# A decoder block on one core: attention scores over all 128 rows, another order within the attention step, query halves, and other buffers for some weights

## The chip, the core and the metric

The kernel runs on one core of a Trainium2 chip. A core has a matrix engine (TensorE, in the profile PE, its weight loads PEld), a vector engine (VectorE, DVE), a scalar engine (ScalarE, ACT), GpSimd (POOL) and a queue that issues transfers (SyncE, SP). The metric is the device time of one execution in microseconds. The kernel before takes 1441.95 us, the median of three runs (1440.77 to 1442.16).

## What is computed

One decoder layer on 1024 tokens of width 1024, in float32:

```python
u = rmsnorm(x, norm_mix_w)
proj = u @ w_in + b_in
cb, cc, cx, q, k, v, g_conv, g_attn = split(proj)
y_conv = (cb * causal_dwconv(cc * cx, conv_mix_w)) @ w_conv_out
q, k = apply_rope(q, cos, sin), apply_rope(k, cos, sin)
y_attn = sliding_window_attention(q, k, v, sinks) @ w_attn_out + b_attn_out
x = x + (sigmoid(g_conv) * y_conv + sigmoid(g_attn) * y_attn) @ w_mix_out
u = rmsnorm(x, norm_ffn_w)
up, gate = split(u @ w_ffn_up)
x = x + (silu(causal_dwconv(up, ffn_conv_w, ffn_conv_b)) * gate) @ w_ffn_down
return rmsnorm(x, norm_final_w)
```

The attention has 8 query heads of 64 channels and 2 key heads, blocks of 128 queries that see their own and the previous block of keys, a mask inside these 256 keys, and a learned sink per head in the denominator:

```python
scores = where(valid, q @ k.T * scale, -inf)
m = maximum(max(scores), sink)
p = exp(scores - m)
probs = p / (sum(p) + exp(sink - m))
```

## The kernel before, in words

Every float32 product is made from two parts of each operand: the first is the value rounded to the matrix engine's format (ScalarE copies it), the second the remainder (VectorE subtracts). `mm3` (L142) multiplies first by first, first by second and second by first, so a product of a 128 by 128 weight block with 512 tokens is three matmuls. The stages follow each other: an opening with norm, transposes of u and the first parts of the key and query projections; the rest of the projections for q, k and v; the attention; its output projection (`ya`); the other input projections, the convolution's and the gates' (`Pairs`, with sums of blocks so that seven products do the work of eight); the convolution's output (`yc`); the mixing product; and the feed-forward part.

In the opening the order of all engines is written out by hand. `load_x` asks for a block of 128 tokens, `rows_of` norms it, `cols_of` transposes it and splits it into u's parts, `part` multiplies a quarter of the tokens, `turn_on(n)` does the next n instructions of the tables for the rotary embedding on VectorE and GpSimd, `keep_warm` are matmuls of zeros.

Queries lie in two tiles `qs[0]` and `qs[1]`, one per key head g. A tile holds on the 64 rows of its own head the first parts and on the other 64 rows the second parts of the same queries, for four heads of the group (c). `ks[g]` holds the first parts of its keys twice, on both row halves. So one matmul over 128 rows gives first by first and second by first. The remaining term, first parts of the queries by second parts of the keys, is a matmul over the 64 own rows with `kl`, one tile whose two halves belong to the two key heads (L444 and L445).

The attention has 16 steps, one for each query block n and key head g (`Step`). What a step does is spread over three turns of the loop, and the order of TensorE, ScalarE and VectorE in it is again written by hand (`manual_schedule`). In turn i TensorE computes the scores of step i + 1, the transposes of the probabilities of step i, half of a filler (a product of the input projection that fills the time, 24 matmuls, L144 to L146) and the values of step i. VectorE takes the maxima of step i + 1 head by head (L451, with the reading of the accumulator), negates all four (L454), adds the sinks (L455), totals step i - 1 (L495), takes the second parts of the probabilities (L139 with `pl`), stores the second parts of the output (L139 with `qs`), and norms step i + 1 (L465 to L467); in every second turn it also takes the second parts of the next filler's weights. ScalarE computes the first parts (`ph`), the exponentials (L460, one per head, and L461 for the sink), the rest of the output (L491), its first parts, and in every second turn a filler's eviction (L430) and weights.

Tiles come from pools: `act` has 16 buffers of 4 KB per row, `tmp` 2, `rawp` 2 for weights as they land, `ps` 4 accumulators of two banks. An instruction that needs a buffer waits for the last reader of what was in it. SP issues its transfers in order, so one that waits for a buffer holds those behind it. Outside the hand-written stretches a scheduler sets the order; `issue_after` puts an instruction behind a given one. `tail_in` loads the convolution's output weights (`load_co`) and the z tiles (`load_z`) during the last products of the input projections.

## Time and profile before

| what | value |
|---|---|
| median of three runs | 1441.95 us |
| profiled execution, its own time | 1441.58 us |
| its span | 1439.8 us |
| TensorE busy | 1418.2 us (98%) |
| VectorE busy | 1003.6 us (70%) |
| ScalarE busy | 562.5 us (39%) |
| GpSimd busy | 85.7 us (6%) |
| mean granted clock of TensorE | 0.997 of full speed |

The span goes from the first to the last instruction, and the execution's own time includes what lies around it. Busy time is the time in which at least one instruction of the engine runs. [...] In a list of waits a row names who waited, for what, and how long in total.

### The profile page before, as it was taken

The numbers are of one execution on the slowest core, as the hardware profiler recorded it, in microseconds if no ns is written. First come the engines' busy times: TensorE is split into PE (matmuls) and PEld (weight loads), VectorE is DVE, ScalarE is ACT, GpSimd is POOL, SyncE is SP. The second block draws the span as 40 slices with busy tenths as digits, with TensorE's granted clock in tenths as the row PEclk, the third lists the DMA queues.
The fourth block names the chain that finished last, engine by engine and source line by source line (L and its number), as shares of the span: only waits on it lengthen the run. The fifth ranks groups of instructions, "written<-read, shape, count | busy, mean of one in ns | idle before, by whom it ended". The sixth has DMA issues, their size and how long they took to land.

```text
span 1439.8 us, 17099 instructions
## 1 busy us (share of the span) xinstructions
PE 1418.2 (98%) x6447; PEld 1164.9 (81%) x6447; DVE 1003.6 (70%) x1511; ACT 562.5 (39%) x897; POOL 85.7 (6%) x144
## 2 busy tenths in 40 slices
PE   8999999999999999999999999999999999999997
PEld 6987777788888888877888878888888888888886
DVE  7575676856788787545644697787777777655567
ACT  5545555623333333232323543333333334444343
POOL 5210000000000000000000000000000000000000
PEclk9999999999999999999999999999999999999999
DMA  5320000242455554255552222222232225797603
GB/s 217 89 59 30 30 16 30 88 161 74 161 205 205 191 185 178 76 177 196 184 174 103 74 98 107 101 105 95 88 110 93 99 94 197 275 377 256 195 31 146
DMA packets 68450, 193.18 MB, mean 134 GB/s; under 512 B 8144, under 2 KB 8400, under 8 KB 68368
## 3 DMA queue, kind: packets, MB, share of 16 engines
q1 hardware_dynamic: 53280, 139.64, 28.8%
q0 software_dynamic: 14368, 51.13, 9.2%
q10 hardware_dynamic: 720, 1.33, 0.3%
q8 instruction: 50, 0.82, 0.2%
q14 instruction: 32, 0.26, 0.1%
HBM read 136.75 MB, written 52.69 MB: 132 GB/s over the span
## 4 chain that ended last, share of the span: by engine, by line
PE 86%; DVE 6%; DMA 5%; ACT 2%; issue 1%; SPq 0%; DVEq 0%; ACTq 0%
PE xup L649 8%; PE zup L649 8%; PE yup L649 8%; PE dna L1151 8%; PE dnb L1151 6%; PE yin L649 5%; PE xin L649 5%; PE zin L649 5%; PE wup L649 4%; PE win L649 3%; PE ps_fill L144 3%; PE ps_fill L146 3%; PE ps_fill L145 3%; PE mx L145 2%; PE mx L146 2%; PE mx L144 2%
## 5 line engine op out<-in xcount | busy, mean ns | idle before, releaser
L1138 DVE TENSOR_TENSOR pd<-rd,pd 128x1024 fp32r<-128x1024 f32 x77 | 93.7, 1222 | 54.1 <-ACT pd L1141 50.3
L627 ACT CAST pup<-sup 128x512 fp32r<-128x512 f32 x80 | 47.8, 620 | 203.2 <-DVE sup L613 203.2
L1141 ACT CAST pd<-rd 128x1024 fp32r<-128x1024 f32 x77 | 80.6, 1053 | 104.1 <-PE dnb L1151 37.1
L1151 PE MATMUL dna<-pd 128*128 128x512 f32 x528 | 120.3, 389 | 0.0
L1151 PEld LDWEIGHTS dna<-pd 128*128 128x128 f32 x528 | 99.1, 188 | 20.5
L1151 PE MATMUL dnb<-pd 128*128 128x512 f32 x396 | 90.2, 389 | 0.0
L1151 PEld LDWEIGHTS dnb<-pd 128*128 128x128 f32 x396 | 74.3, 188 | 15.4
L649 PE MATMUL zin<-u,pin 128*128 128x512 f32 x360 | 86.1, 389 | 0.0
L627 ACT CAST pin<-sin 128x512 fp32r<-128x512 f32 x52 | 31.1, 620 | 135.3 <-DVE sin L613 126.4
L649 PEld LDWEIGHTS zin<-u,pin 128*128 128x128 f32 x360 | 67.6, 188 | 14.0
L630 DVE TENSOR_TENSOR pup<-sup,pup 128x512 fp32r<-128x512 f32 x80 | 53.6, 689 | 18.5 <-ACT pup L627 15.0
L144 PE MATMUL ps_fill<-u,w_fill 128*128 128x512 f32 x160 | 64.0, 400 | 0.0
L146 PE MATMUL ps_fill<-u,w_fill 128*128 128x512 f32 x160 | 62.5, 391 | 0.0
L145 PE MATMUL ps_fill<-u,w_fill 128*128 128x512 f32 x160 | 62.3, 389 | 0.0
L649 PE MATMUL yup<-b22h,pup 128*128 128x512 f32 x176 | 57.9, 390 | 0.9 <-DVE aup L665 0.9
L649 PE MATMUL zup<-b11h,pup 128*128 128x512 f32 x176 | 57.8, 390 | 0.0
L649 PE MATMUL zup<-b21h,pup 128*128 128x512 f32 x176 | 57.7, 389 | 0.0
L451 DVE CUSTOM_DVE_ANT_0 p<-s,cst_sb,pcol_sb 128x256 f32<-128x256 f32 x64 | 27.2, 480 | 37.2 <-PE s L445 34.6
L649 PE MATMUL yup<-bt1h,pup 128*128 128x512 f32 x160 | 52.5, 389 | 0.0
L649 PE MATMUL wup<-bt2h,pup 128*128 128x512 f32 x160 | 52.5, 389 | 0.0
L649 PE MATMUL xup<-bt3h,pup 128*128 128x512 f32 x160 | 52.5, 389 | 0.0
L649 PE MATMUL xup<-bt4h,pup 128*128 128x512 f32 x160 | 52.5, 389 | 0.0
(361 smaller groups left out, 3470.4 us busy)
## 6 DMA issues: line engine op xcount, KB each, us to landing
rup<-in_w_up SPq DMA_DIRECT2D x44, 512.0 KB, 3.5
rin<-in_w_in SPq DMA_DIRECT2D x30, 512.0 KB, 6.7
td<-in_w_down SPq DMA_DIRECT2D x22, 512.0 KB, 5.3
tsp<-td POOLq DMA_DIRECT2D x22, 512.0 KB, 3.7
rd<-tsp SPq DMA_DIRECT2D x44, 256.0 KB, 5.3
rd<-in_w_down SPq DMA_DIRECT2D x33, 256.0 KB, 5.3
rd<-hs SPq DMA_DIRECT2D x33, 256.0 KB, 3.7
x<-in_x SPq DMA_DIRECT2D x16, 512.0 KB, 3.7
```

The costliest lines, as they stand in the source:

```text
L144: nc.tensor.matmul(dst, ah, bh, start=first, stop=False)
L145: nc.tensor.matmul(dst, ah, bl, start=False, stop=False)
L146: nc.tensor.matmul(dst, al, bh, start=False, stop=last)
L451: nc.vector.tensor_tensor_reduce(out=self.p[:, c], in0=self.s[:, c], in1=masks[0 if self.n == 0 else 1], scale=SCALE, scalar=pc(COL_SINK + ...
L627: nc.scalar.copy(self.parts[p, q][:, 0], src())
L630: v.tensor_sub(t[:, 1], src(), t[:, 0].bitcast(F32))
L649: nc.tensor.matmul(dst, a, b[:, kc], start=first and i == 0, stop=last and i == 2, skip_group_check=p >= PLAIN and more)
L1138: v.tensor_sub(t[:, 2:], raws_d[n - 1], t[:, :2].bitcast(F32))
L1141: nc.scalar.copy(parts_d[n][:, :2], raws_d[n])
L1151: nc.tensor.matmul(sets[side, i], t[:, s, tok], t[:, b], start=g == 0 and k == 0 and not more, stop=g == NG - 1 and k == 2, skip_group_che ...
```

## The change

Scores: `kl` becomes two tiles, one per key head, whose other 64 rows GpSimd fills with zeros; the second score matmul runs over all 128 rows with the same stationary queries as the first. The first gate block is written to DRAM after its eviction and read again behind the attention. Query block 0 has no previous keys: its transposes, parts and values go over one block of keys in place of two. Queries lie in two halves of 512 tokens, and the first two blocks of the output projection are multiplied half by half. In the step, each head's maximum is followed by its negation, the exponentials of the next step stand ahead of the first parts, and the norms ahead of the second parts. The last filler's product moves into the hand-written order, and sums that the scheduler had put ahead of the last total are issued behind the attention. The convolution's output weights 1 to 3 and the first z tiles land in `act` buffers, the weights asked for earlier. In the opening, loads, table work and parts change their places.

```diff
@@ opening (order written out by hand) @@
         load_x(0)
+        load_x(1)
...
-        load_x(1)
...
         raw_k = load_unit(w_in[U_K], "k")
+        raw_q0 = load_unit(w_in[U_Q], "q0")
...
-        turn_on(2)
         rows_of(0)
-        turn_on(1)
         rows_of(1)
+        turn_on(8)
         cols_of(0, False)
         keep_warm(N_WARM[1])
+        early["k"] = split_unit(raw_k, "k", eng=nc.gpsimd)
         cols_of(0, True)
-        early["k"] = split_unit(raw_k, "k", eng=nc.gpsimd)
-        turn_on(5)
         cols_of(1)
+        turn_on(20)
...
-    qs = [mid(f"qs{g}", F32R) for g in range(2)]
+    qs = [mid(f"qs{g}", F32R, (P, 2, 4, 512)) for g in range(2)]
     ks = [act(f"ks{g}", F32R) for g in range(2)]
-    kl = act("kl", F32R)
+    kl = [act(f"kl{g}", F32R) for g in range(2)]
+    for g in range(2):
+        nc.gpsimd.memset(kl[g][other[g]].bitcast(F32), 0.0)
...
-            split(k[own[g]], ks[g][own[g]], kl[own[g]])
+            split(k[own[g]], ks[g][own[g]], kl[g][own[g]])
...
+    gsp0 = dram.tile([P, T], F32, name="gsp0")
...
+        nc.scalar.activation(filled[f], ps_fill[f], AF.Identity, bias=pc(COL_BIN + col))
+        if f == 0:
+            nc.gpsimd.dma_start(gsp0, filled[f])
...
+            self.blocks = 2 if self.n else 1
...
             for c in range(4):
-                nc.tensor.matmul(self.s[:, c], qs[g][:, c, self.queries], ks[g][:, kc], start=True, stop=False)
-                nc.tensor.matmul(self.s[:, c], qs[g][rows, c, self.queries], kl[rows, kc], start=False, stop=True)
+                nc.tensor.matmul(self.s[:, c], qs[g][:, self.h, c, self.queries], ks[g][:, kc], start=True, stop=False)
+                nc.tensor.matmul(self.s[:, c], qs[g][:, self.h, c, self.queries], kl[g][:, kc], start=False, stop=True)
...
-            nc.vector.tensor_scalar_mul(st[:, 1], st[:, 0], -1.0)
+                nc.vector.tensor_scalar_mul(st[:, 1, c:c + 1], st[:, 0, c:c + 1], -1.0)
...
-            for k2 in range(2):
+            for k2 in range(self.blocks):
...
-        def split(self):
+        def first_parts(self):
             self.hl = [act(f"p{x}{self.name}", F32R, (P, 2, 4, P)) for x in "hl"]
-            split(self.pt, *self.hl)
+            nc.scalar.copy(self.hl[0][:, :self.blocks], self.pt[:, :self.blocks])
+        def second_parts(self):
+            hi, lo = [x[:, :self.blocks] for x in self.hl]
+            nc.vector.tensor_sub(lo, self.pt[:, :self.blocks], hi.bitcast(F32))
...
+            n = 2 * self.blocks
+            for i in range(n):
...
-            step.split()
             if nxt:
                 nxt.exps()
+            step.first_parts()
             fill_part(f, h, range(KC))
-            if nxt is st[-1]:
+            if nxt:
                 nxt.norms()
+            step.second_parts()
             if prev:
                 prev.store()
-            if nxt and nxt is not st[-1]:
-                nxt.norms()
...
+        nc.vector.scalar_tensor_tensor(filled[8], ps_fill[9], pc(COL_BIN + U_X), filled[8], op0=ALU.add, op1=ALU.mult)
         st[-1].rest()
...
+    gas[0] = act("ga0")
+    nc.sync.dma_start(gas[0], gsp0)
...
-            next(gen_in)
-            next(gen_in)
+            with tc.issue_after(after_attention):
+                next(gen_in)
+                next(gen_in)
...
+        yas = [ps(f"ya{2 * q + jj}") for jj in range(2)]
+        for jj, h in [(jj, h) for h in range(2) for jj in range(2)] if q == 0 else [(jj, h) for jj in range(2) for h in range(2)]:
+            for c in range(4):
+                f = slice((jj * 4 + c) * P, (jj * 4 + c + 1) * P)
+                mm3(yas[jj][:, halves[h]], wa[q][0][:, f], wa[q][1][:, f], qs[0][:, h, c], qs[1][:, h, c], c == 0, c == 3)
...
+    def fetch_co(n):
+        raws_co[n] = act(f"raw_co{n}")
+        nc.sync.dma_start(raws_co[n], w_co[n // 2, n % 2])
...
-        for f in {0: [lambda: load_co(0)], 1: [lambda: load_z(0, 0)], 2: [lambda: load_z(0, 1)], 3: [lambda: load_co(1)],
-                  5: [lambda: load_co(2)], 6: [lambda: load_z(0, 2), lambda: load_z(0, 3)], 7: [lambda: load_co(3)]}.get(m, ()):
+        for f in {0: [lambda: load_co(0)], 1: [lambda: load_z(0, 0), lambda: fetch_co(1)], 2: [lambda: load_z(0, 1), lambda: fetch_co(2)],
+                  3: [lambda: load_co(1)], 4: [lambda: fetch_co(3)],
+                  5: [lambda: load_co(2), lambda: load_z(0, 2)], 6: [lambda: load_z(0, 3)], 7: [lambda: load_co(3)]}.get(m, ()):
```

VectorE, from the last maximum of a turn to the store of the output, in the kernel before (p are the probabilities, sm the statistics of the step's four heads, pt the transposed probabilities, pl their second parts, os and o the output):

```order
L451 ISA p_1195,sm_1196<-s_1175,cst_sb,pcol_sb 128x256
L451 ISA sm_1196 128x1
L454 TENSOR_SCALAR sm_1196<-sm_1196 128x4
L455 TENSOR_TENSOR sm_1196<-sm_1196,pcol_sb 128x4
L495 TENSOR_TENSOR os_1184<-o_1170,os_1184 64x512
L139 TENSOR_TENSOR pl_1205<-pt_1186,ph_1204 128x1024
L139 TENSOR_TENSOR qs_705<-os_1184,qs_704 64x4x128
L465 TENSOR_TENSOR sm_1196<-sm_1196 128x4
L466 RECIPROCAL sm_1196<-sm_1196 128x4
L467 TENSOR_TENSOR p_1195<-p_1195,sm_1196 128x1024
```

The same stretch of VectorE in the changed kernel, from the third head on:

```order
L457 ISA p_1276,sm_1277<-s_1254,cst_sb,pcol_sb 128x256
L457 ISA sm_1277 128x1
L460 TENSOR_SCALAR sm_1277<-sm_1277 128x1
L457 ISA p_1276,sm_1277<-s_1254,cst_sb,pcol_sb 128x256
L457 ISA sm_1277 128x1
L460 TENSOR_SCALAR sm_1277<-sm_1277 128x1
L461 TENSOR_TENSOR sm_1277<-sm_1277,pcol_sb 128x4
L506 TENSOR_TENSOR os_1265<-o_1249,os_1265 64x512
L471 TENSOR_TENSOR sm_1277<-sm_1277 128x4
L472 RECIPROCAL sm_1277<-sm_1277 128x4
L473 TENSOR_TENSOR p_1276<-p_1276,sm_1277 128x1024
L487 TENSOR_TENSOR pl_1294<-pt_1267,ph_1293 128x1024
```

The three rows of the norms (L465 to L467 before, L471 to L473 now) moved from behind the store to ahead of the second parts, and a negation of one column stands behind every head.

ScalarE, from the rest of an output to the first parts of the stored one in the kernel before (ph are the first parts of the probabilities):

```order
L491 COPY os_1263<-o_1245 64x512
L138 CAST ph_1283<-pt_1265 128x1024
L460 ACTIVATE p_1274,sm_1275<-p_1274,sm_1275 128x256 x4
L461 ACTIVATE sm_1275<-sm_1275 128x4
L138 CAST qs_704<-os_1263 64x4x128
```

The same five rows of ScalarE's step in the changed kernel, with its line numbers:

```order
L502 COPY os_1265<-o_1249 64x512
L466 ACTIVATE p_1276,sm_1277<-p_1276,sm_1277 128x256 x4
L467 ACTIVATE sm_1277<-sm_1277 128x4
L483 CAST ph_1293<-pt_1267 128x1024
L138 CAST qs_704<-os_1265 64x4x128
```

The exponentials of the next step moved ahead of the first parts of this one.

## Rows read from the trace of the kernel before

**Rows 1.** The page: busy us, share of span, instructions; then the chain's shares.

```profile
PE 1418.2 (98%) x6447; PEld 1164.9 (81%) x6447; DVE 1003.6 (70%) x1511; ACT 562.5 (39%) x897; POOL 85.7 (6%) x144
...
PE 86%; DVE 6%; DMA 5%; ACT 2%; issue 1%; SPq 0%; DVEq 0%; ACTq 0%
```

**Rows 2.** Waits of TensorE: line, releaser, us in total, times, longest.

```profile
PE tp_a L182 <- DVE y_a L172: 3.6, 4, 1.6
PE yc L144 <- ACT co L138: 1.9, 1, 1.9
...
PE ya L144 <- ACT qs L138: 1.0, 1, 1.0
```

**Rows 3.** Stretches: us, busy by engine (instructions), granted clock, DMA share, GB/s.

```profile
0.00:20.00 20.00, 13.91 (x65) 7.76 (x66) 12.94 (x30) 10.97 (x18) 6.32 (x9) 1.00 0.78 286
...
160.00:180.00 20.00, 20.00 (x92) 15.45 (x91) 14.03 (x37) 11.12 (x27) 0.00 (x0) 1.00 0.11 34
```

**Rows 4.** Timeline of TensorE, one attention step: start, us, engine, line, operation.

```profile
146.74 0.28 PE L444 MATMUL s<-ks,qs 128*128 128x256 f32 x1
146.95 0.38 PE L445 MATMUL s<-kl,qs 64*128 64x256 f32 x1
147.26 0.38 PE L444 MATMUL s<-ks,qs 128*128 128x256 f32 x1
...
149.13 1.09 PE L473 MATMUL pt<-cst_sb,p 128*128 128x128 f32 x8
149.98 0.48 PE L144 MATMUL ps_fill<-u,w_fill 128*128 128x512 f32 x1
...
155.53 0.39 PE L483 MATMUL o<-ph,vs 128*128 128x512 f32 x1
```

**Rows 5.** Chain of waits, one query part in the opening: start, us, count.

```profile
36.30 2.87 PE ps_q L288 x24
```

**Rows 6.** Timeline of the weight loads in the same stretch.

```profile
36.03 2.94 PEld L288 LDWEIGHTS ps_q<-u,w_q 128*128 128x128 f32 x24
```

**Rows 7.** Timeline of VectorE in the step before that of rows 4.

```profile
140.74 0.48 DVE L451 CUSTOM_DVE_ANT_0 p<-s,cst_sb,pcol_sb 128x256 f32<-128x256 f32 x1
141.15 0.08 DVE L451 DVE_READ_ACCUMULATOR2_ANT sm<- 128x1 f32 x1
141.27 0.17 DVE L454 TENSOR_SCALAR sm<-sm 128x4 f32<-128x4 f32 x1
141.47 0.16 DVE L455 TENSOR_TENSOR sm<-sm,pcol_sb 128x4 f32<-128x4 f32 x1
141.66 0.69 DVE L495 TENSOR_TENSOR os<-o,os 64x512 f32<-64x512 f32 x1
142.39 1.23 DVE L139 TENSOR_TENSOR pl<-pt,ph 128x1024 fp32r<-128x1024 f32 x1
144.38 0.69 DVE L139 TENSOR_TENSOR qs<-os,qs 64x512 fp32r<-64x512 f32 x1 [0.77 <-ACT qs L138]
145.08 0.16 DVE L465 TENSOR_TENSOR sm<-sm 128x4 f32<-128x4 f32 x1
...
145.50 1.22 DVE L467 TENSOR_TENSOR p<-p,sm 128x1024 f32<-128x1024 f32 x1
```

**Rows 8.** Timeline of VectorE in the opening: two small instructions.

```profile
9.40 0.15 DVE L156 TENSOR_SCALAR st_a<-ss_a 128x1 f32<-128x1 f32 x1
9.47 0.16 DVE L157 RECIPROCAL st_a<-st_a 128x1 f32<-128x1 f32 x1
```

**Rows 9.** Groups of the attention stretch, by form: the exponentials; mean ns.

```profile
L460 ACT ACTIVATE p<-p,sm 128x256 f32<-128x256 f32 x64 | 31.8, 499 | 6.3 <-DVE sm L454 6.2
```

**Rows 10.** Timeline of VectorE behind the attention.

```profile
271.00 2.35 DVE L740 TENSOR_TENSOR ta<-u 128x1024 f32<-128x1024 f32 x2
...
275.65 0.69 DVE L495 TENSOR_TENSOR os<-o,os 64x512 f32<-64x512 f32 x1
```

**Rows 11.** DMA issues near the convolution's output weights: count, KB, us to landing.

```profile
raw_co<-in_w_co SPq DMA_DIRECT2D x7, 512.0 KB, 3.6
```

More of the change, by code (lines that the diff above doesn't have):

```diff
@@ L324, in hybrid_kernel @@
         nc.sync.dma_start(cst_sb[:, CST_MASK:], cst[:, CST_MASK:])
+        early["q0"] = split_unit(raw_q0, "q0")
         rows_of(2)
-        turn_on(20)
-        early["q0"] = split_unit(raw_q0, "q0")
+        part("k", 0)
         rows_of(3)
-        part("k", 0)
+        part("q0", 0)
         cols_of(2)
@@ L332, in hybrid_kernel @@
         rows_of(4)
-        part("q0", 0)
         cols_of(3)
+        part("q1", 0)
         rows_of(5)
-        part("q1", 0)
+        cols_of(4)
         part("k", 1)
-        cols_of(4)
         rows_of(6)
+        cols_of(5)
         part("q0", 1)
-        cols_of(5)
         rows_of(7)
-        turn_on(4)
+        cols_of(6)
         part("q1", 1)
-        part("k", 2)
-        cols_of(6)
-        turn_on(7)
-        part("q0", 2)
         cols_of(7)
         turn_on()
+        part("k", 2)
+        part("q0", 2)
         part("q1", 2)
@@ L393, in rope_queries @@
         for g in range(2):
-            split(q[own[g]], qs[g][own[g], c], qs[g][other[g], c])
+            split(q[own[g]].rearrange("p (h t) -> p h t", h=2), qs[g][own[g], :, c], qs[g][other[g], :, c])
     turn = {"k": rope_load(ps_early["k"], COL_BIN + U_K, "k")}
@@ L435, in __init__ @@
             self.name = f"{self.n}{self.g}"
-            self.queries = slice(self.n * P, (self.n + 1) * P)
+            self.h, self.queries = self.n // 4, slice(self.n % 4 * P, (self.n % 4 + 1) * P)
+            self.blocks = 2 if self.n else 1
         def scores(self):
-            rows, g = own[self.g], self.g
+            g = self.g
             w0 = max(0, self.n - 1) * P
@@ L481, in values @@
             self.o = ps(f"o{self.name}", (P, 4, P))
-            for i in range(4):
-                nc.tensor.matmul(self.o, vs[self.g][:, n0 + i // 2], self.hl[i % 2][:, i // 2], start=i == 0, stop=i == 3)
+            n = 2 * self.blocks
+            for i in range(n):
+                nc.tensor.matmul(self.o, vs[self.g][:, n0 + i // 2], self.hl[i % 2][:, i // 2], start=i == 0, stop=i == n - 1)
         def rest(self):
@@ L715, in hybrid_kernel @@
     c_0 = filled[8]
-    v.scalar_tensor_tensor(c_0, ps_fill[9], pc(COL_BIN + U_X), c_0, op0=ALU.add, op1=ALU.mult)
-    conv_taps(0, c_0)
+    with tc.issue_after(after_attention):
+        conv_taps(0, c_0)
     units_in = [(U_GC, U_B)]
@@ L789, in hybrid_kernel @@
                 nc.scalar.activation(gas[j], gas[j], AF.Sigmoid)
-            ya = ps(f"ya{j}")
-            for cols in halves:
-                for c in range(4):
-                    f = slice((jj * 4 + c) * P, (jj * 4 + c + 1) * P)
-                    mm3(ya[:, cols], wa[q][0][:, f], wa[q][1][:, f], qs[0][:, c, cols], qs[1][:, c, cols], c == 0, c == 3)
-            v.scalar_tensor_tensor(ms[j], ya, pc(COL_BAO + j), gas[j], op0=ALU.add, op1=ALU.mult)
+            v.scalar_tensor_tensor(ms[j], yas[jj], pc(COL_BAO + j), gas[j], op0=ALU.add, op1=ALU.mult)
             nc.gpsimd.dma_start(msp[j], ms[j])
@@ L851, in steps_in @@
                 3: [(2, lambda p: gate(p, bank("z"), pin.uv[p][:, 0]))]}.get(q, [])
-    wco, zparts = {}, {}
+    wco, zparts, raws_co = {}, {}, {}
     def load_co(n):
         gr, hc = n // 2, n % 2
-        raw = load_unit(w_co[gr, hc], f"co{n}")
+        raw = raws_co.pop(n) if n in raws_co else load_unit(w_co[gr, hc], f"co{n}")
         wco[gr, hc] = blk(blkc[0] if n < 7 else blka, f"co{n}", F32R, (P, 2, 1024))
         split(raw, wco[gr, hc][:, 0], wco[gr, hc][:, 1])
+    def fetch_co(n):
+        raws_co[n] = act(f"raw_co{n}")
+        nc.sync.dma_start(raws_co[n], w_co[n // 2, n % 2])
     def load_z(th, k):
-        raw = rawp.tile([P, 512], F32, name=f"zr{th}{k}", tag="raw")
+        raw = rawp.tile([P, 512], F32, name=f"zr{th}{k}", tag="raw") if th or k > 3 else act(f"zr{th}{k}", F32, (P, 512))
         nc.sync.dma_start(raw, zsp[k][:, halves[th]])
```

12 lines of the change are left out of this document (6 added, 6 removed).

## Prediction, on record before the changed kernel ran

> **What bounds the kernel now.** I read the page's busy lines and its chain first. TensorE is busy for 1418.2 of 1439.8 us and holds 86% of the chain [rows 1], so a change counts only by the TensorE time that it takes away, or by the 21.6 us in which that engine stood idle. The list of its waits names part of this idle time: 3.6 us on normed rows in the opening, 1.9 us on the convolution's output weights, 1.0 us on the last attention output [rows 2]. [...] A full engine can still be slow, so the next view is TensorE's timeline in one attention step. A step runs from the first score at 146.74 to the next: eight score matmuls, eight transposes from 149.13, 24 filler matmuls from 149.98, four value matmuls from 155.53 [rows 4]. The scores take 2.39 us, and they are where the change works.
>
> **The change part by part.** The sum is made against the profiled execution, 1441.58 us; the median is 1441.95, 0.4 above.
>
> *Scores over all rows.* Each head's scores are a full-row matmul (128\*128) and one over 64 rows (64\*128). Except for the first, they start 0.31 us apart, though each streams only 256 columns [rows 4]. Full-row matmuls of the same 256 columns stand in the opening: 24 in 2.87 us, 0.120 each [rows 5]. What the two differ in is the switch between 128 and 64 rows at every instruction; the change ends it, since the second matmul now reads all rows, with zeros in half of the key remainders. I take 8 x 0.120 = 0.96 in place of 2.39: 1.43 per step, 16 steps, 22.9 us. Bounds: the transposes start 0.85 / 8 = 0.106 apart [rows 4], which would add 1.7 us to the gain; at an unchanged 0.31 the gain is nothing. The ps_q row is nearest, since it has the columns, the type and the rows.
>
> [...]
>
> *Query block 0.* Its two steps lose the block ahead of the sequence: four of eight transposes (4 x 0.106 = 0.42) and two of four value matmuls (2 x 0.227, the distance of filler matmuls: (155.53 - 149.98) / 24 = 0.23). 0.88 per step, 1.8 us in all.
>
> *The order within a step.* Negation now follows each head's maximum, the exponentials stand ahead of the first parts on ScalarE, and on VectorE the division (norms) stands ahead of the second parts. Before, the second parts started at 142.39 and the values over two us after their end; now everything in the chain scores, maxima, exponentials, norms, second parts must end before the value matmuls, in a step that is shorter by 1.43 us. From the first score (0): the scores end at 0.84 + 0.28 = 1.12, so maxima start near 1.16. A head costs 0.41 (140.74 to 141.15), 0.12 until the next small instruction can start, and then between 0.07 and 0.20 until the one behind it: 0.07 is the distance of two independent small instructions, 0.20 that of the negation and the addition that depends on it [rows 7, 8]. So four heads take 2.4 to 2.9. The addition 0.19, the total 0.73, the norms 1.64 (145.08 to 146.72), the second parts 1.23 [rows 7]: they end at 7.35 to 7.87. ScalarE is not later: the last exponential, 0.50 [rows 9], begins at the last negation and ends while addition and total (0.92) still run. TensorE asks for the second parts at 0.96 + 0.85 + 5.55 + 0.23 = 7.59. The wait is thus 0 to 0.28 plus some 0.05 for the signal, the middle 0.07; over the 14 steps with four values 1.0 us, range 0 to 4.6. Queued behind the waiting value matmul are the next scores, so a wait lengthens the step in full. As a sum VectorE has 6.9 to 7.4 per step with the 0.70 of the store, and 1.23 more for a filler's weights in every second one: 7.5 to 8.0 on the mean, against 8.27 of TensorE. It fits, with little to spare; the cover that hid all this before, over two us between second parts and values, is gone.
>
> *After the attention.* Before, the scheduler put two token sums ahead of the last total: 271.00 to 275.65 on VectorE, and the output projection waited 1.0 us for the last store [rows 2, 10]. Now these sums are held behind the attention, and the first projection does the first query half for two output blocks (24 x 0.227 = 5.4 us) before it needs the last store. The multiplication that is now ahead of the last total costs VectorE 1.3, which lies inside these 5.4. Gain 1.0, bounds 0 and 1.3. The sums lose some five us of lead; they are wanted by the products behind the projection, which itself lasts 192 x 0.227 = 44 us.
>
> *The spill.* The first gate block goes to DRAM and comes back before its sigmoid; this pays for the second tile of key remainders. SP gets one more issue ahead of the first weights of the next stage, and POOL's queue one in the attention, where it is idle (0.00 us) [rows 3]. The block is read by ScalarE, and TensorE gets to the fifth projection before it needs a bank that hangs on it: 0. If that cover failed, it would be one transfer, 3.6 us [rows 11]. POOL's two zero fills stand ahead of the key's half swaps; I take 0, for VectorE and not these copies was last ahead of the scores.
>
> *Convolution output weights.* Three of these blocks now land in activation buffers, asked for earlier, and four z tiles with them, where two raw buffers were shared. The wait of 1.9 on ACT co [rows 2] should go: 1.9. Against it, SP issues in order, and a fetch that waits for an activation buffer holds up what is behind it; the price of one such miss is a landing, 3.6 us [rows 11]. Bounds -1.9 and +3.
>
> *Opening.* The second row block is asked for ahead of the norm gain, the table work goes behind the first two row blocks, the first query part ahead of two transposes. The DMA engines were 0.78 busy there [rows 3] and the bytes stay, and VectorE has as much to do as before: by its order the norms of two row blocks end near 11.3 us, the eight table instructions near 15, and two remainders of u (1.23 each, as in rows 7) near 17.5, where the third part of the key product waits for them as it did. I take 0. Bounds: 2.0 gained (the 3.6 us of tp_a without its longest, 1.6 [rows 2]) to 2.0 lost (its longest and a bit once more).
>
> The sum: -22.9 - 1.8 + 1.0 - 1.0 - 1.9 = -26.6. From 1441.58 this is 1415.0, from the median 1415.3; I say **1415**.
>
> **The rivals.**
> *VectorE's chain is late.* If each negation costs its full 0.20, a head takes 0.73, the second parts end at 7.87 and values wait 0.33: 14 x 0.33 = 4.6 instead of 1.0, and the time is 1418.6. For it: the negation and its addition stand 0.20 apart [rows 7]; against: two small instructions 0.07 apart [rows 8]. [...]
> *The scores stay slow.* The 0.31 is not the switch of rows but the weight loads, or the many short groups. Then the first term is gone: 1441.6 - 3.7 = 1437.9, and the step's cover stays, so the 1.0 goes too: about 1437. Against it: transposes change their group at each instruction and stand 0.106 apart.
> *Slower.* The chain is serial now. If a head's maximum, negation and exponential take turns between the engines, its length sets the step. To eat all 26.6 us the second parts must come 26.6 / 14 = 1.9 later than I say, so a head must cost 0.67 + 1.9 / 4 = 1.15 in place of 0.67; from there on the kernel is slower, at 1.25 per head 1447. Nothing in rows 7 comes near 1.15.
>
> **How the numbers follow.** Forecast 0.74, late chain 0.16, slow scores 0.06, slower 0.03, and 0.01 for something else. 0.2% is 2.9 us, about what a measurement tells from no change; slow scores at 1437 lie outside that, though a stall would bring them in. Faster 0.95, same 0.02, slower 0.03. The forecast's own ends: 1415 less 1.7 (0.106), 2.0 (opening) and 1.0 (no wait) is 1410; the late chain with a lost 2.0 in the opening, a lost gain of 1.9 and half a missed landing is 1424. The bounds do not all come together, so 1408.5 to 1424 holds 8 in 10 with both cases in it.
>
> **What would show it.** In the profile after: score matmuls 0.12 apart and transposes 0.96 after the first score; 16 scores taking 15 and not 38 us; the wait of values on pl (VectorE) at most 0.1 per step, or 0.3 where the rival holds; a head on VectorE at 0.6 to 0.73; no wait of ya on qs; a yc wait without co; the opening's first 20 us near 13.9 busy. Wrong if scores stay 0.3 apart, if steps grow over 8.6 us, or if a new wait over 3 us stands in the opening or at yc.

## The result and the profile after

The changed kernel takes 1417.94 us, the median of four runs (1414.77 to 1419.77), beside 1441.75 us for the kernel before: a ratio of 0.9834, 95% interval 0.9815 to 0.9852. It is 1.7% faster, inside the forecast's range, and 2.9 us above the 1415 that were forecast. The profiled execution took 1419.77 us, the longest of the four, so the stages below, which are cut from it, add up to 1.8 us more than the median would.

The page answers to [rows 1]: TensorE has lost 26.5 us of busy time, but the span only 22.1 (1439.8 to 1417.7). The first two lines are the busy line and the chain's shares of the kernel after.

```profile
PE 1391.7 (98%) x6435; PEld 1157.3 (82%) x6435; DVE 1007.5 (71%) x1559; ACT 565.2 (40%) x897; POOL 87.6 (6%) x147
...
PE 86%; DVE 6%; DMA 4%; ACT 2%; issue 1%; SPq 0%; DVEq 0%; ACTq 0%
```

The difference is time in which TensorE stands, and its list of waits (line, releaser, us in total, times, longest) shows where, beside [rows 2]:

```profile
PE tp_a L182 <- DVE st_a L156: 3.8, 2, 2.6
PE mx L144 <- ACT mx L138: 3.7, 1, 3.7
PE ps_k L288 <- DVE u L139: 2.7, 1, 2.7
...
PE ya L144 <- ACT qs L138: 0.9, 1, 0.9
PE mx L145 <- DVE mx L139: 0.8, 1, 0.8
PE o L494 <- DVE pl L487: 0.7, 1, 0.7
```

The waits at yc are gone, and mx, which waited 0.2 us before, waits 3.7 + 0.8 us; the opening's waits have grown; ya's is still there. To see what this is worth I cut each span at TensorE's first matmul of a stage (first score `s`, first `ya`, `xin`, `yc`, `mx`, `zup`) and subtract. All kernels of this document, in us; the first seven columns are stages, and their sum is the span of the profiled execution:

| kernel | opening, projections | attention | ya | input projections | yc | mx | rest | median of the runs |
|---|---|---|---|---|---|---|---|---|
| before | 109.6 | 160.9 | 45.5 | 285.6 | 98.9 | 99.4 | 639.9 | 1441.75 |
| after | 112.8 | 136.6 | 45.0 | 285.6 | 92.5 | 105.3 | 639.9 | 1417.94 |
| scores64 | 111.6 | 160.1 | 45.0 | 285.6 | 92.5 | 105.0 | 639.9 | 1441.84 |
| before128 | 109.5 | 136.9 | 45.5 | 285.6 | 98.3 | 99.3 | 640.0 | 1418.00 |
| order_old | 112.9 | 135.2 | 45.0 | 285.6 | 92.5 | 103.5 | 639.8 | 1416.67 |
| block0_full | 112.7 | 138.3 | 45.1 | 285.5 | 92.5 | 100.5 | 639.8 | 1417.41 |
| open_old | 109.6 | 136.5 | 45.0 | 285.6 | 92.5 | 105.1 | 639.9 | 1414.69 |
| open_mid | 111.6 | 136.5 | 46.6 | 285.8 | 92.5 | 106.1 | 639.9 | 1420.41 |
| gm_more | 112.9 | 136.6 | 45.1 | 285.6 | 92.4 | 98.9 | 639.9 | 1413.62 |
| sums_late | 113.0 | 136.5 | 43.5 | 285.6 | 92.5 | 106.3 | 639.8 | 1418.42 |
| tail_gm | 112.8 | 136.5 | 45.1 | 285.6 | 99.7 | 103.7 | 639.9 | 1425.94 |
| best_neworder | 109.6 | 136.5 | 43.5 | 285.6 | 92.5 | 100.2 | 639.8 | 1408.06 |
| best | 109.5 | 135.2 | 43.5 | 285.6 | 92.5 | 98.6 | 639.9 | 1407.25 |
| best_open | 113.1 | 135.2 | 45.0 | 285.8 | 92.5 | 98.6 | 639.9 | 1411.09 |

So the attention gained 24.3 us. Two other stages moved by as much as 6 us and all but cancelled: yc gained 6.4 and mx lost 5.9. The opening lost 3.2, ya gained 0.5. Each row of the table is one execution, and a stage can differ between rows although its code is the same: with the opening of after 111.6 to 113.0 us, and in mx, with after's loads and two buffers, 100.5 to 106.3. Both are taken up below.

**The attention.** TensorE's timeline of one step (start, us, engine, line, operation) answers to [rows 4]:

```profile
142.14 0.28 PE L450 MATMUL s<-ks,qs 128*128 128x256 f32 x1
142.25 0.28 PE L451 MATMUL s<-kl,qs 128*128 128x256 f32 x1
...
143.09 1.04 PE L479 MATMUL pt<-cst_sb,p 128*128 128x128 f32 x8
143.88 0.47 PE L144 MATMUL ps_fill<-u,w_fill 128*128 128x512 f32 x1
...
149.65 0.39 PE L494 MATMUL o<-pl,vs 128*128 128x512 f32 x1
...
150.35 0.28 PE L450 MATMUL s<-ks,qs 128*128 128x256 f32 x1
```

The scores stand 0.12 apart, though each lasts 0.28, so what one costs is read from the starts and not from its duration. The transposes start 0.95 us after the first of them, where it was 2.39. What goes with the 0.31 us of before shows in the weight loads of the step of [rows 4] (a note in brackets is the idle time ahead of the row and what ended it; `issue` is nothing that the profile shows):

```profile
146.95 0.18 PEld L445 LDWEIGHTS s<-kl,qs 64*128 64x128 f32 x1 [0.24 <-issue]
147.26 0.19 PEld L444 LDWEIGHTS s<-ks,qs 128*128 128x128 f32 x1
```

Each load starts together with its own matmul (146.95 and 147.26), the second 0.31 behind the start of the one ahead; 0.19 for a load and the 0.12 of a full-row matmul add up to that. After, every matmul still has its load:

```profile
142.25 0.19 PEld L450 LDWEIGHTS s<-ks,qs 128*128 128x128 f32 x1
142.37 0.19 PEld L451 LDWEIGHTS s<-kl,qs 128*128 128x128 f32 x1
```

Their matmuls start at 142.37 and 142.49, so these loads run beside the matmul ahead of theirs. This step is 8.21 us long (142.14 to 150.35); every second step, in which a filler's weights stand ahead of VectorE's maxima, is 8.30. VectorE's timeline of the step shown answers to [rows 7]:

```profile
143.29 0.48 DVE L457 CUSTOM_DVE_ANT_0 p<-s,cst_sb,pcol_sb 128x256 f32<-128x256 f32 x1 [1.28 <-PE s L451]
143.70 0.08 DVE L457 DVE_READ_ACCUMULATOR2_ANT sm<- 128x1 f32 x1
143.81 0.15 DVE L460 TENSOR_SCALAR sm<-sm 128x1 f32<-128x1 f32 x1
143.88 0.47 DVE L457 CUSTOM_DVE_ANT_0 p<-s,cst_sb,pcol_sb 128x256 f32<-128x256 f32 x1
...
148.23 1.22 DVE L487 TENSOR_TENSOR pl<-pt,ph 128x1024 fp32r<-128x1024 f32 x1
```

A head costs 0.59 us from maximum to maximum; the next maximum starts 0.07 after the negation, though the negation lasts 0.15. The second parts end at 149.45 and the matmul that reads them starts at 149.65, so here nothing waits for them.

### The profile page after: what moved, and what is told of

Its sections match the earlier page's. It is cut to its first block, busy times and chain, and to the rows that moved or that the text cites. A ratio compares the mean times of both kernels' runs of the same rounds, so it can differ in the third digit from the quotient of the medians.

```text
span 1417.7 us, 17129 instructions
## 1 busy us (share of the span) xinstructions
PE 1391.7 (98%) x6435; PEld 1157.3 (82%) x6435; DVE 1007.5 (71%) x1559; ACT 565.2 (40%) x897; POOL 87.6 (6%) x147
## 4 chain that ended last, share of the span: by engine, by line
PE 86%; DVE 6%; DMA 4%; ACT 2%; issue 1%; SPq 0%; DVEq 0%; ACTq 0%
PE xup L662 8%; PE zup L662 8%; PE yup L662 8%; PE dna L1171 8%; PE dnb L1171 6%; PE yin L662 6%; PE xin L662 6%; PE zin L662 6%; PE wup L662 4%; PE win L662 3%; PE ps_fill L144 2%; PE ps_fill L146 2%; PE ps_fill L145 2%; PE mx L145 2%; PE mx L146 2%; PE mx L144 2%
## 5 line engine op out<-in xcount | busy, mean ns | idle before, releaser
L144 PE MATMUL mx<-mx,m 128*128 128x512 f32 x128 | 50.9, 398 | 3.7 <-ACT mx L138 3.7
```

Source lines behind the costliest of these rows:

```text
L144: nc.tensor.matmul(dst, ah, bh, start=first, stop=False)
```

## The experiments

Each is the changed kernel with one edit, but for before128, which is the kernel before with one, tail_gm, which adds one to gm_more, and the three kernels at the end, which join several.

**scores64: the row change taken back alone.**

```diff
-nc.tensor.matmul(self.s[:, c], qs[g][:, self.h, c, self.queries], kl[g][:, kc], ...)
+nc.tensor.matmul(self.s[:, c], qs[g][own[g], self.h, c, self.queries], kl[g][own[g], kc], ...)
```

> The changed kernel, with only the second score product of each pair back on the 64 rows of its own key group. Theory (the pace between products of 128 and of 64 rows is what was paid): eight products a step again take 2.39 us instead of 0.96, 16 steps, so +22.9 us less the 0.7 that the values now wait: about 1440 us. Rival (the gain comes from the new order in a step, the per-head exponentials and the halved query layout, which all stay): within 3 us of 1418 us.

Measured: 1441.84 us, ratio to before 0.9999 (0.9988 to 1.0011): the whole gain of the change is gone. The score matmuls of this kernel (min/median/max ns, first and last start, form):

```profile
L450 PE MATMUL s<-ks,qs x64: 276/384/388, 111.6 to 255.6; 128*128 128x256 f32 x64
L451 PE MATMUL s<-kl,qs x64: 378/381/383, 111.8 to 255.9; 64*128 64x256 f32 x64
```

The full-row matmuls, which were not touched, are slow again too (median 384 ns), because each stands behind one of 64 rows. The attention takes 160.1 us, 23.5 more than after.

**before128: the row change put into the old kernel alone.**

```diff
-nc.tensor.matmul(self.s[:, c], qs[g][rows, c, self.queries], kl[rows, kc], ...)
+nc.tensor.matmul(self.s[:, c], qs[g][:, c, self.queries], kl[:, kc], ...)
```

> The kernel before, with only the second score product of each pair taken over all 128 rows of its queries and of the low key parts; the other group's low parts are then added to the scores, which the reference does not have. Theory (the row change alone carries the gain, and the old order has cover: the probabilities are ready 0.7 us before the next transposes): -22.9 us, about 1419 us. Rival (the new order is needed: with the shorter step the multiply of the probabilities comes late in each step): gains under 16 us, 1426 us or more, and TensorE waits for p in nearly every step.

Measured: 1418.00 us, ratio 0.9838 (0.9822 to 0.9855), the time of the changed kernel. The score matmuls:

```profile
L444 PE MATMUL s<-ks,qs x64: 277/283/283, 109.5 to 231.6; 128*128 128x256 f32 x64
L445 PE MATMUL s<-kl,qs x64: 282/283/283, 109.7 to 231.7; 128*128 128x256 f32 x64
```

The attention gained 24.0 us (160.9 to 136.9) in the old order of a step, with one negation for all heads and both key blocks for the first queries. With scores64 this shows the cause from both sides: what cost the time is the alternation of 128 and 64 rows. No run puts products of 64 rows behind each other, so how fast those would be isn't shown. All other parts of the change, whatever each is worth, add up to nothing in the medians.

**order_old: the old order inside a step.**

```diff
+            step.first_parts()
+            step.second_parts()
             if nxt:
                 nxt.exps()
-            step.first_parts()
             fill_part(f, h, range(KC))
-            if nxt:
+            if nxt is st[-1]:
                 nxt.norms()
-            step.second_parts()
             if prev:
                 prev.store()
+            if nxt and nxt is not st[-1]:
+                nxt.norms()
```

> The changed kernel with the old order inside a step: both parts of the probabilities ahead of the exponentials, the norms behind the store; scores over all rows and the negation per head stay. Theory (both orders have cover): the low parts come 1.5 us earlier, the multiply ends some 0.7 us ahead of the next transposes, so TensorE waits for neither: -0.7 to 0 us, 1417.2 to 1417.9 us. Rival (the order was needed for the short step): the multiply is late by 0.3 us or more in each of 16 steps, +5 us or more, 1423 us.

Measured: 1416.67 us, ratio 0.9827 (0.9812 to 0.9842). By the time alone this is no difference from after; the attention tells it: 135.2 us against 136.6, with no wait of TensorE in it. VectorE's timeline of this kernel in a step shows the cover that the old order has:

```profile
146.72 1.23 DVE L487 TENSOR_TENSOR pl<-pt,ph 128x1024 fp32r<-128x1024 f32 x1
...
148.97 1.22 DVE L473 TENSOR_TENSOR p<-p,sm 128x1024 f32<-128x1024 f32 x1
```

The second parts end at 147.95 for a matmul at 149.70, the probabilities at 150.19 for transposes at 151.34. Both have over a microsecond to spare, so the new order wasn't needed for the shorter step; it costs 1.4 us. Of these 0.6 lie ahead of the last step's scores, where every second step takes 8.30 us instead of 8.22, and 0.8 behind, with the wait of 0.7 us for the second parts that the list of after shows (once, at 241.31 us).

**block0_full: both key blocks for the first queries again** (`self.blocks = 2` in all steps).

> The changed kernel with both key blocks for the first query block again. Theory: two steps get four transposes and two value products back, 0.92 us each, all on TensorE's path: +1.8 us, 1419.7 us. Rival (in the first steps TensorE waits for the chain of VectorE anyway): 0 us, with a wait of the first steps shorter by what is added.

Measured: 1417.41 us, ratio 0.983 (0.9815 to 0.9844), and by the time this would be the rival. By the stage it is the theory: the attention takes 138.3 us, 1.7 more. The time doesn't show it because mx, whose code is the same, took 100.5 us instead of 105.3 in this kernel; its long wait came out short:

```profile
PE mx L144 <- ACT mx L138: 0.4, 1, 0.4
```

That wait is 3.7 us after, 1.9 in order_old, 3.6 in sums_late. It seems to depend on how transfers fall: the load of the last mixing weights is issued 4.9 us ahead of mx's first matmul after, and 7.7 in block0_full; why, no run shows. It hides any edit of a microsecond or two ahead of it. Hence the next edit.

**gm_more: more buffers for the merges of the second token half.** In the mix's stage the convolution's output is multiplied with a gate and added to the attention's (`merge`); both are loaded into a `tmp` buffer, of which there are two. The edit puts the odd ones into blocks that the convolution weights have left.

```diff
-        gm = tmp(f"gm{th}{j}", F32, (P, 2, 512))
+        gm = blk(blkc[0], f"gm{th}{j}", F32)[:, :2] if th and j % 2 else tmp(f"gm{th}{j}", F32, (P, 2, 512))
```

> The changed kernel with the odd merges of the second token half in blocks that the convolution weights have left, so that eight merges share six buffers and not two. Theory (the stage of the mix lost 6 us because the loads of the merges queue for two buffers, and the last weights are converted behind them on ScalarE): the mix's stage, from its first product to the first product of the up projection, takes 99.5 to 100.5 us instead of 105.3, TensorE's 3.7 us wait there is under 1 us and the clock of 680 to 690 us is 1.00; 4 to 5 us faster, 1413 to 1414 us. Rival (the last weights wait for their block or their load): the wait stays over 3 us, and the time within 1 us of 1418 us.

Measured: 1413.62 us, ratio 0.9809 (0.9795 to 0.9822). mx takes 98.9 us in place of 105.3, and the list of waits no longer has it. After, ScalarE's timeline shows what the wait was:

```profile
680.38 0.62 ACT L138 CAST m<-gm 128x512 fp32r<-128x512 f32 x1 [2.32 <-DVE gm L938]
684.23 0.62 ACT L138 CAST m<-gm 128x512 fp32r<-128x512 f32 x1 [3.23 <-DVE gm L938]
684.75 1.04 ACT L138 CAST mx<-raw_mx 128x1024 fp32r<-128x1024 f32 x1
```

and VectorE's, one step further back:

```profile
682.35 0.69 DVE L937 TENSOR_TENSOR gm<-yc,gm 128x512 f32<-128x512 f32 x1 [2.08 <-DMA gm<-gsp]
```

The last mixing weights are converted on ScalarE behind a merge; the merge waits for its load, the load for one of two buffers. The stretches (us, busy by engine with instructions, granted clock, DMA share, GB/s) of after show that the wait costs more than itself, since the clock that was granted falls:

```profile
680.00:690.00 10.00, 5.58 (x18) 3.99 (x17) 5.34 (x8) 2.19 (x3) 0.00 (x0) 0.84 0.46 157
```

The same stretch of gm_more:

```profile
680.00:690.00 10.00, 10.00 (x46) 8.29 (x45) 6.56 (x13) 2.08 (x4) 0.53 (x1) 1.00 0.52 160
```

Waits of 3.7 + 0.8 us made the stage 6.4 us longer. Taken by the microsecond, the granted clock of after is 1.00 up to 686 us, 0.50 from 687 to 690 and 1.00 again from 691; from 687.70 to 689.83 the matmuls start 0.43 us apart, where they start 0.23 apart from 690.25 on.

**tail_gm: gm_more with the convolution weights and z tiles loaded as before** (the two raw buffers shared, nothing asked for earlier).

```diff
-        raw = raws_co.pop(n) if n in raws_co else load_unit(w_co[gr, hc], f"co{n}")
+        raw = load_unit(w_co[gr, hc], f"co{n}")
...
-        raw = rawp.tile([P, 512], F32, name=f"zr{th}{k}", tag="raw") if th or k > 3 else act(f"zr{th}{k}", F32, (P, 512))
+        raw = rawp.tile([P, 512], F32, name=f"zr{th}{k}", tag="raw")
```

> The changed kernel with the merges in six buffers, and the loads of the first convolution weights and z parts in the order that they had before. Theory (the new order of these loads gained 6 us in the convolution output, which the merges then gave back; without that loss it stays): the convolution output takes 98.3 us again instead of 92.4, the mix 99 us, and the time is 5 to 6 us above the kernel with the merges alone, 1419 us. Rival (the loads of the convolution weights are hidden, and the stage gained by something else): 1413.6 us, the convolution output at 92.4 us.

Measured: 1425.94 us, ratio 0.9895 (0.9882 to 0.9909), 12.3 above gm_more, twice what I expected. yc takes 99.7 us (7.3 more), and mx 103.7 (4.8 more), so the late loads are felt in the next stage too. Its waits of TensorE there:

```profile
PE yc L144 <- ACT co L138: 2.4, 1, 2.4
PE mx L144 <- ACT mx L138: 2.0, 1, 2.0
...
PE yc L144 <- ACT z L138: 0.8, 1, 0.8
PE mx L145 <- DVE mx L139: 0.8, 1, 0.8
```

In their own stage the earlier loads are worth 7 us, far more than the wait on co that the list of before showed (1.9 us, [rows 2]). In before there are smaller waits beside it (1.1 us for gm and 0.4 for z in the same list), and the clock fell behind it, as the stretch shows in which that wait lay:

```profile
630.00:640.00 10.00, 8.61 (x31) 6.96 (x32) 3.83 (x4) 3.33 (x4) 0.00 (x0) 0.83 0.50 157
```

The clock is not the main part. In before128 it is 1.00 in all of yc, the waits in the list sum to 3.2 us, and the stage still takes 98.3 us, 5.8 more than after. Such a list counts only the time in which the engine stands idle: around a wait that it gives as 1.24 us the matmuls start 1.63 us apart (643.75 and 645.38), where 0.23 is the pace.

With the merges in two buffers the same loads were worth nothing in the profiled execution of after: yc and mx together take 197.8 us, and 197.6 in before128, which has the old loads. So the stage's gain was handed on, in full there and in part in block0_full, where the two take 193.0. Why mx is slower in tail_gm than in before128 (99.3) isn't settled; the other buffers also change the order in which SP issues the transfers of this stretch.

**sums_late: the token sums truly behind the attention.** After, VectorE's timeline behind the attention reads as in [rows 10], sums first:

```profile
249.89 2.35 DVE L753 TENSOR_TENSOR ta<-u 128x1024 f32<-128x1024 f32 x2
252.16 2.35 DVE L753 TENSOR_TENSOR tc<-u 128x1024 f32<-128x1024 f32 x2
254.54 0.69 DVE L506 TENSOR_TENSOR os<-o,os 64x512 f32<-64x512 f32 x1
```

The instruction behind which the change holds them is ScalarE's part of the last store; VectorE's own queue isn't held by it. The edit names VectorE's part of the same store.

```diff
+        split.second = (eng or nc.vector).tensor_sub(lo, src, hi.bitcast(F32))
...
+        after_total = split.second.ins    # VectorE's subtraction of the last store
...
-            with tc.issue_after(after_attention):
+            with tc.issue_after(after_total):
                 next(gen_in)
                 next(gen_in)
```

> The changed kernel with the four token sums held behind VectorE's last store of the attention, where the changed kernel holds them behind ScalarE's half of that store only. Theory (they are what the last total stands behind, from 249.9 to 254.5 us): the last total runs 4.6 us earlier, the 0.9 us wait of the attention's output projection is gone, -0.9 us, and nothing else moves. Rival (the sums then stand ahead of the remainder of the second weights or of the next stage's parts): the projection waits there instead, 0 to +2 us.

Measured: 1418.42 us, ratio 0.9837 (0.9824 to 0.9851). ya takes 43.5 us instead of 45.0, and its wait is gone: 1.5 us, somewhat more than expected. The time doesn't show it, for mx took 106.3.

**open_old: the opening in the order of before** (the whole hand-written stretch).

> The changed kernel with the opening's work in the order that it had before. Theory (the new opening loses 3.2 us up to the first score, as the two traces show, whatever follows): the first score starts at 109.6 us again instead of 112.8, and the time falls by 3.2 us, to 1414.7 us. Rival (the loss comes from the rest of the change, from the two clearings of the low key parts on GpSimd or the halved query layout, which stay): the first score starts at 112 us or later and the time doesn't change.

Measured: 1414.69 us, ratio 0.9813 (0.98 to 0.9827), the first score at 109.6 us. The loss is the opening's own. What is late there shows in TensorE's timeline of after:

```profile
13.22 2.18 PE L288 MATMUL ps_k<-u,w_k 128*128 128x256 f32 x16
18.11 2.08 PE L288 MATMUL ps_k<-u,w_k 128*128 128x256 f32 x8 [2.71 <-DVE u L139]
19.98 3.59 PE L288 MATMUL ps_q<-u,w_q 128*128 128x256 f32 x24
```

and in VectorE's:

```profile
10.88 2.33 DVE L209 CAST posf<-posi 128x8 f32<-128x8 int32 x1
...
15.36 0.43 DVE L217 TENSOR_TENSOR rt<-rt 128x256 f32<-128x256 f32 x1
15.70 2.35 DVE L139 TENSOR_TENSOR u<-tp_a,u 128x1024 fp32r<-128x1024 f32 x2
```

The key product's third part waits for u's remainders, which stand behind the table work. A long table instruction is not new: before, a subtraction of 128x256 (L213) lasted 2.50 us there beside GpSimd's split of the key weights, but it stood between the two remainders. The second of them ended at 17.62 us then and ends at 18.05 now. Behind the wait eight matmuls start 0.23 us apart (18.11 to 19.98), twice the 0.12 of [rows 5], and the granted clock from 18 to 20 us was 0.50.

The pace doesn't fall in every execution. In scores64, with the same opening and the same wait, the eight matmuls took 1.22 us and not 2.08:

```profile
18.03 1.22 PE L288 MATMUL ps_k<-u,w_k 128*128 128x256 f32 x8 [2.71 <-DVE u L139]
```

There the first score starts at 111.6 us. So 1.2 of the 3.2 us came with the slow matmuls, and 2.0 without them.

**open_mid: the first eight table steps behind the two remainders of u.**

```diff
-        turn_on(8)
         cols_of(0, False)
...
         cols_of(1)
-        turn_on(20)
+        turn_on(28)
```

> The changed kernel with one thing of its opening moved: the first eight steps of the rope tables stand on VectorE behind the first two remainders of u, not ahead of them. Theory (the conversion of the positions, 2.33 us on VectorE beside GpSimd's work, holds the remainders up, and the stall costs the granted clock too): the 2.7 us wait of the first part of k shrinks under 1 us, the granted clock stays at 1.00 from 15 to 30 us, and the first score starts 2 to 3 us earlier, about 1415.5 us. Rival (the order of the token loads decides: the later rows come late anyway, and a stall of as much follows at the transposes of rows 2 to 4): the first score within 0.7 us of 112.8 us.

Measured: 1420.41 us, ratio 0.9849 (0.9835 to 0.9862). The first score starts at 111.6 us, so 1.2 of the 3.2 came back, between theory and rival. The granted clock was 1.00 from 15 to 30 us, as expected; it fell earlier (0.91 over the first 20 us). But 111.6 is also where scores64 stands, whose opening is unchanged and whose matmuls kept their pace, so this run doesn't show that the move itself gained anything. The wait on u is gone, and others have come at the next places, among them these:

```profile
PE tp_a L182 <- DVE st_a L156: 3.9, 3, 2.3
PE tp_a L182 <- DVE y_a L172: 1.4, 1, 1.4
...
PE ps_q L288 <- DVE w_q L139: 1.0, 1, 1.0
```

The time got worse by mx (106.1) and by a new wait of 1.4 us of xin for VectorE's reading of the last ya. Behind the opening the order of the instructions is the same as in after; where this wait comes from stays open.

**best and best_neworder: the edits together.** best has the edits of open_old, gm_more, sums_late and order_old; best_neworder the first three.

> The changed kernel with four edits of the runs so far together: the old opening, the odd merges in six buffers, the token sums behind the attention, the old order inside a step. Theory (each worth lies in a stage of its own, so they add): 3.3 for the opening, 4.3 for the merges, 1.4 for the sums, 1.4 for the order, together 10 us, about 1408 us. Rival (a later stage takes some of it back, as the mix did from the convolution output): 1411 us or more, with a wait of TensorE longer than in the runs before.

> The same without the fourth edit: the changed kernel's own order inside a step, its wait of the values on the low parts with it. Theory (the old order is worth 1.4 us on top, as its stage showed): 1.4 us above the kernel with all four, about 1409.5 us, the attention 136.6 us from the first score to the first output projection against 135.2. Rival (the order is worth nothing outside the one stage's last steps): no more than 0.5 us between the two.

Measured: best 1407.25 us, ratio to before 0.9766 (0.9752 to 0.9779), below both kernels; best_neworder 1408.06, 0.9773 (0.9759 to 0.9786). The stages add as expected. The order's worth is 1.3 in the attention (136.5 to 135.2), the time's difference of 0.8 alone wouldn't show it. Of TensorE's waits the opening's are left in best, and one of 0.9 us in the up projection:

```profile
PE tp_a L182 <- DVE y_a L172: 3.9, 4, 1.7
PE ps_k L288 <- DVE st_a L156: 1.5, 1, 1.5
```

**best_open: can the new opening be mended?** best, with the new opening and its 28 first table steps behind q1's weights.

```diff
-        turn_on(8)
...
-        turn_on(20)
...
         early["q1"] = split_unit(raw_q1, "q1")
+        turn_on(28)
         rows_of(4)
```

> The kernel with all four edits, but the opening is the changed kernel's own with all 28 first table steps moved behind the second query weights' remainder, so that two remainders of u, the weights' and two norms stand ahead of them. Theory (the new opening is late because VectorE does table work while TensorE waits for remainders and weights, and by nothing else in it): no wait of the first parts of k and q over 0.3 us, the granted clock at 1.00 from 13 us on, the first score at 107.5 to 109 us, earlier than with the old opening (109.5), and 1406 to 1407 us. Rival (the loads' order and the early q0 part cost by themselves): the first score at 110.5 us or later, as in the kernel where only eight steps were moved (111.6). Third possibility: the tables, 22 us of GpSimd's work that now starts near 25 us, end too late for their transposes at 52 us, and the wait stands there.

Measured: 1411.09 us, ratio 0.9782 (0.9768 to 0.9795), the first score at 113.1 us: none of the three came true as a whole; the rival's time did, but the long wait below is for VectorE and not for a load. TensorE's timeline:

```profile
13.25 3.14 PE L288 MATMUL ps_k<-u,w_k 128*128 128x256 f32 x24
16.23 3.04 PE L288 MATMUL ps_q<-u,w_q 128*128 128x256 f32 x24
...
29.64 1.97 PE L182 MATMUL tp_a<-cst_sb,y_a 128*128 128x128 f32 x8 [3.84 <-DVE st_a L156]
31.26 4.68 PE L288 MATMUL ps_k<-u,w_k 128*128 128x256 f32 x24
```

The first parts of k and q run without a wait; q's starts at 16.23 us where it started at 19.98 after. Then the work that was put off is due at once, one wait of 3.8 us takes the place of several small ones, and 24 matmuls behind it take 4.68 us instead of 3.1. From 26 to 30 us VectorE is busy for 3.80 of the 4.00 and TensorE for 0.36: here moving VectorE's work moved the wait. Of the 5.3 us by which this span is longer than that of best, the opening has 3.6; the other 1.7 stand in ya and the input projections, with the same wait of 1.4 us of xin as in open_mid, which stays open here too.

## Why the prediction was right, and where it wasn't

| term | predicted | measured | from |
|---|---|---|---|
| scores over all rows | -22.9 | -24.0 | before128, attention |
| query block 0 | -1.8 | -1.7 | block0_full, attention |
| order within the step | +1.0 | +1.4 | order_old, attention |
| after the attention (ya) | -1.0 | -0.5 | the two traces |
| spill of the gate | 0 | none seen | the two traces |
| convolution output weights (yc) | -1.9 | -6.4 | the two traces |
| the mix (mx) | not in the sum | +5.9 | the two traces |
| opening | 0 | +3.2 | open_old |
| sum | -26.6 | -22.1 | profiled spans |

The last row compares after's longest execution; between the medians it is -23.8.

*Scores.* Right, in mechanism and size: the pace of full-row matmuls in the opening [rows 5] carried over to the scores. Most of the 1.1 us on top are the transposes: behind scores of all rows the eight of a step take 0.79 us up to the filler (143.09 to 143.88), where they took 0.85 [rows 4], and in before128 that is 0.9 us in 15 steps. The rival of slow scores put the 0.31 down to the weight loads or the many short groups. After has as many loads and as many groups, 0.12 us a matmul: loads of all rows run beside matmuls of all rows, as in [rows 5, 6], and it was between 64 and 128 rows that each load started with its own matmul, 0.31 us a matmul. So the distance of 0.12 in after, and the median durations in before128 (283 ns for both forms, 384 and 381 in scores64), refute this rival.

*Query block 0 and the order.* The first is right. The order's 1.4 is near the 1.0 of the sum, but less than half of it is the small wait in the steps that I priced: about 0.08 us in every second step. The wait of 0.7 us at the values of the last step but one was no term, so that the sizes meet is in part luck. VectorE's head cost 0.59 us, just under the 0.6 to 0.73 that I gave, since the next maximum starts 0.07 after the negation. The late chain, 0.33 us in each of 14 steps, didn't come. That the new order buys nothing I hadn't said: I priced its stall and left the question whether it was needed.

*After the attention.* The step "now these sums are held behind the attention" failed. I took it from the change's words; the order of VectorE's instructions, which was there to be read, still has them ahead of the last total. sums_late shows that the rest of the reasoning held: with the sums really behind, the wait goes. The 0.5 that ya gained all the same is for the most part another wait, of 0.3 us for w_ao, which the list of after no longer has.

*Convolution output weights.* The direction was right, the size was not: 6.4 for 1.9. I took one row of the waits for the stage's loss. The stage had smaller waits beside it and slow starts behind them that no list shows; a granted clock of 0.83 came on top, but before128 lost 5.8 us there without it. And I didn't ask what waits next when yc ends 6 us sooner: the merges, whose loads share two buffers, and behind them the last mixing weights. gm_more and tail_gm show that the gain is real and was handed on.

*Opening.* The step that failed is "VectorE has as much to do as before". It has, but the order decides which of its instructions TensorE waits for, and I gave no price to one long wait against several short ones. My arithmetic put the remainders' end near 17.5 us, which was nearly right (18.05), and went on "where the third part of the key product waits for them as it did". It ended its wait only 0.4 us later than before (18.11 for 17.67). But TensorE was there sooner, so the wait was 2.7 us in one piece and not 1.5; the slow matmuls that stood behind it in this execution (0.23 us apart, granted clock 0.50) were no term at all, nor were the waits further on for u and for the norms (1.3 and 1.2 us). The loss of 3.2 lay outside the bound of 2.0; with matmuls at their pace, as in scores64, it would have been at it.

The forecast came within 2.9 us because errors of both signs met: 1.1 more from the scores, 4.5 more from yc, against 5.9 in mx and 3.2 in the opening. That is luck, the more so since the last two differ between executions of the same code. Of the signs, the pace of the scores, the transposes and yc came as said. The wait of ya on qs did not go, the first 20 us were busy for 12.8 us and not near 13.9, and the new wait over 3 us stood at mx, which I had not named.

## What to carry to other kernels

When two kinds of matmul alternate, look at the distance of their starts: here the scores over half of the rows, between those over all, stood 0.31 us apart, and over all rows, with zeros in the unused half, 0.12; the half-row ones also slowed the full-row ones behind them (median 384 ns for 282). Price the removal of a wait by the stage, from its first instruction to the next stage's, not by its row in the list, and ask at once what the next stage will wait for. Where a stage's wait hangs on how transfers fall, edits of a microsecond or two can't be read from the total time; cut the span into stages, or mend that wait first.

## What the runs showed of the hardware

- A matmul of 128 rows behind one of 64, and the reverse, starts 0.31 us after it, for 256 columns (0.21 in the first pair of a step) [rows 4]; 128 behind 128 starts 0.12 us after. In the first case the load starts with its own matmul (147.26 in before), in the second beside the one ahead (at 142.25 in after, for a matmul at 142.37). In scores64 the full-row ones slow down with the others (median 384 ns against 282).
- Behind a wait of 2.7 us in the opening of after, eight matmuls stood 0.23 us apart; behind one of 3.7 in mx the ten microseconds were granted 0.84; behind one of 3.8 in best_open 24 matmuls took 4.68 us instead of 3.1. The length of a wait doesn't settle it: in scores64 eight matmuls took 1.22 us behind the same 2.7 us. In best, whose four waits of tp_a in the opening sum to 3.9 us with 1.7 the longest, the granted clock was 1.00 from 0 to 40 us; in best_neworder, with the same opening and three such waits of 4.0 us, 2.2 the longest, a matmul of ps_q lasted up to 561 ns (388 in best), and the first score came 0.1 us later. In mx 4.5 us of waits cost 6.4.
- A conversion of 128x8 on VectorE lasted 2.33 us (10.88 us, above) while GpSimd ran a subtraction of 128x1024 from 10.10 to 13.18; in open_mid, with GpSimd idle, the same conversion lasted 0.16. In before the 128x256 subtraction L213 lasted 2.50 us (from 12.66) beside the same work of GpSimd (12.52 to 14.88), and 0.43 after.
